# Up projection of a gated MLP: nineteen seven-product block pairs in eight column groups instead of sixteen in eleven, more split buffers, and a residual copy in eight pieces

## The chip, the cores and the metric

One core of a Trainium2 chip runs the whole kernel. The metric is device time in microseconds (us) from the start to the end of one execution. The engines named here are TensorE (PE, matrix products; PEld is its weight load), VectorE (DVE), ScalarE (ACT), GpSimd (POOL) and SyncE (SP, which here mostly issues DMA transfers). The program lists each engine's instructions in one fixed order; at an instruction whose data or buffer isn't there yet, the engine waits, and with it all that stands behind.

## The reference

One layer of a decoder trunk with 256 tokens and width 2048, in float32:

```python
h = rms_norm(x, mix_norm_g)
z = h @ w_in                                  # all heads' inputs and gates
ha = mLSTM heads(z); hb = forgetting-attention heads(z)
x = x + concat([ha, hb]) @ w_out              # out projection, 2048 x 2048
h = rms_norm(x, ffn_norm_g)
u = h @ w_up                                  # up projection, 2048 x 11264
a, g = split(u, 2)
a = causal_dwconv(a, conv_w, conv_b)          # width 3, depthwise
x = x + (gelu(a) * g) @ w_down                # down projection, 5632 x 2048
gate = sigmoid(rms_norm(x, ple_norm_g) @ w_ple_gate)
x = x + gate * (p @ w_ple_proj)
```

## The kernel before

**Products in three parts.** Every weight block arrives from HBM in float32 (`raw`). ACT rounds it to the type that the matmuls here take, fp32r (`hi`, line 1292 in the up projection, 295 elsewhere), and DVE subtracts that from the raw block (`lo`, lines 1294 and 297). The activations have been split the same way. Each product is then three matmuls (lines 362 to 364, in `three`): high by high, high by low, low by high. Such a pair of a `hi` and a `lo` is called a split here.

**The up projection in groups.** The 11264 columns are worked in 11 groups `q` = 0 to 10, each of 512 columns of the `a` half and the 512 columns of the `g` half that go with them. A group sums over 16 blocks of 128 rows of `w_up`. A *plain unit* (letter `p` in the table `ORDERS`) takes one block: one transfer of 512 KB, one split of 128x1024, 12 matmuls of 128x512. A *seven* (four units that share a letter, `a` or `b`) takes two blocks together by the seven-product scheme for 2x2 block matrices (Strassen's, in Winograd's form): 21 matmuls in place of 24. Its units have 3, 6, 6 and 6 matmuls; their splits are of 128x512, then three of 128x1024, and DVE forms four sums of raw halves (128x512 each) between them. The products that serve several result blocks gather in PSUM banks `upP`, over all the sevens of a group. At the end of a group with sevens a *combine* follows: one copy by ACT, then two additions and one subtraction on DVE (lines 1762 to 1764), and in the next group two multiply-adds (`summed`, line 1157) that join the combined halves to the plain ones. The activation side of a seven needs sums of left blocks (`S_up`, made once by `up_sums`).

`ORDERS` holds one string of letters for each group, and the units run in the order of the letters. Before, group 0 has two sevens; then groups with one and with two alternate; the last two have one each. That is 16 sevens, and all 11 groups have a combine.

**What sets the order.** `run_units` walks the units. Before the matmuls of unit `i` are listed it lists the splits of units up to `i + AHEAD_UP`, as far as split buffers are free, and the loads as far as raw buffers are free. Before there are eight split buffers (`hi0` to `hi3`, `lo0` to `lo3`) of 128x1024 each. A unit takes two, the first of a seven takes one, and both come free when its matmuls are through. Jobs of the group before (turning the result, line 200; the convolution taps and sums, lines 1176 and 1183; gelu; the product with `g`, line 1189; the split of the result, line 159; for pairs that the down projection treats as sevens their left sums, lines 467 to 471) are hung behind units of the next group, at the places in `TURN_AT` and `ACT_AT`. A scheduler that works at build time puts the instructions in their final order on each engine, by priorities and dependencies.

**The residual.** `xs` holds x after the out projection. `keep_x` copies it to HBM (`kept_x`) by two transfers of 1 MB on SP's queue (line 83): the first behind unit 8 of the second group of the out projection, the second behind unit 8 of the up projection. The out projection also loads its weights through SP (line 286), and ten moves named `mkT<-mkT` (line 206), which bring a transposed tile of the attention heads to its place, go through SP too.

Of the kernel before, what the change touches and what calls it, by code (L numbers as in the profile page):

```python
# [9 lines left out]
F32 = mybir.dt.float32  # L10
# [5 lines left out]
P = 128  # L16
# [19 lines left out]
RAW, PARTS = 3, 4  # L36
AHEAD_UP, AHEAD_LATE = 4, 6

# [19 lines left out]
@with_exitstack  # L58
def layer_kernel(
# [21 lines left out]
    def keep_x(i):  # L81
        c = slice(i * 1024, (i + 1) * 1024)
        nc.sync.dma_start(out=kept_x[:, :, c], in_=xs[:, :, c])

# [182 lines left out]
    def run_stream(blocks, pulls, more, ramp=False):  # L267
# [9 lines left out]
        def put(j):  # L277
            b = blocks[j]
            if b.load is not None:
                b.load()  # L280
            b.raws, b.tags = [], free(j)[: len(b.srcs)]
            for t, src in zip(b.tags, b.srcs):
                held.add(t)
                kb, n = src.shape[1], src.shape[2]
                raw = wp.tile([P, BLK], F32, tag=t, name=f"raw{j}", bufs=1) if t in raw_tags else more[t][2]()
                nc.sync.dma_start(out=raw[:, : kb * n].rearrange("p (k n) -> p k n", k=kb), in_=src)
                b.raws.append(raw)

# [213 lines left out]
    with mixers:  # L502
# [430 lines left out]
        def with_after(b, hook):  # L933
            fn = b.fn
            b.fn = lambda hi, lo: (fn(hi, lo), hook())
# [152 lines left out]
    with tc.tile_pool(name="ffn", bufs=1) as fp:  # L1088
# [62 lines left out]

        def up_turn():

# [7 lines left out]
            def turned(t):  # L1161
# [5 lines left out]
                return f  # L1167
            return [f(t) for t in range(NT) for f in (summed, turned)]

# [34 lines left out]
        now = [0]  # L1204
        spaces = [f"raw{i}" for i in range(RAW)] + [f"{k}{i}" for k in ("hi", "lo") for i in range(PARTS)] + ["v0", "v1", "v2", "v3", "v4"]
# [23 lines left out]
        def space(j, name, kind):  # L1229
# [7 lines left out]
            elif tag == "v4":  # L1237
                v = xs[:, 0, BLK : 2 * BLK]
            elif tag[0] == "v":
                v = spare_raws[f"u{32 + 4 * (i // 2)}"][:, i % 2]  # L1240
# [454 lines left out]
        def up_group(q):  # L1695
# [3 lines left out]

            n7 = "a" in ORDERS[q], "b" in ORDERS[q]  # L1700
            first, n7 = 2 * sum(n7), sum(n7)
            def left(k, t):
# [79 lines left out]
            us = [unit(k) for k in range(first, KD)]  # L1782
            kinds = {"p": iter(us), "a": iter(seven(0)), "b": iter(seven(1))}
            return [next(kinds[c]) for c in ORDERS[q]]

        def up_sums(r):
            f, d = (EZ[:, 0, i * 512 : (i + 1) * 512].rearrange("p (k c) -> p k c", c=256) for i in range(2))
            dve.tensor_add(f, f32(x2[:, 2 * r : 2 * r + 2, 0:256]), f32(x2[:, 2 * r : 2 * r + 2, 256:512]))
            sums_of(f, EZ[:, 1, 0:512].rearrange("p (i c) -> p i c", i=4), S_up[r])

# [28 lines left out]
        for q in range(KF // 4):  # L1819
            for job, i in zip(up_turn(), TURN_AT if q < KF // 4 - 1 else (-1, 0, -1, 1)):  # L1820
                with_after(us[START[q + 1] + i], between(job))
            for i, job in enumerate(up_act(q)):
                if q < KF // 4 - 1:
                    with_after(us[START[q + 1] + ACT_AT[i]], between(job))
                else:
                    with_after(us[first_late + 8 + 2 * i], between(job))
# [33 lines left out]
```

## Time and profile before

| What | Value |
|---|---|
| Median of 3 runs | 1232.29 us (1231.33 to 1235.31) |
| The profiled execution: own time | 1232.22 us |
| The profiled execution: span from first to last instruction | 1230.4 us |
| PE busy | 1223.2 us, 99% of the span |
| DVE busy | 1009.7 us, 82% |
| ACT busy | 757.0 us, 62% |
| Mean granted TensorE clock | 0.999 |

The profile is of one execution, and its own time stands 1.82 us above its span (what lies before the first and behind the last instruction). Busy shares are means over the whole span; a stretch of the timeline has its own.

### The profile page before, as it was taken

The page shows a single profiled execution, that of the slowest core. Times are in us where ns is not written, and L with a number is a line of the kernel's source. Part 1 is how long each engine was busy: PE and PEld are TensorE (multiplying, and loading weights), DVE is VectorE, ACT ScalarE, POOL GpSimd, SP SyncE. Part 2 cuts the span into 40 slices and gives each one's busy share as a digit, 9 for nine tenths or more (in the row PEclk, how much of TensorE's full clock was granted, in tenths as well). Part 3 has the DMA queues.
Part 4 walks back from the last instruction along what each step waited for, and adds up shares of the span by engine and source line. Part 5 has one row for each costly group of instructions (what it writes and reads, how often), then busy time and mean ns, then how long its engine had stood idle before and what let it go on. Part 6 is the DMA issues. An engine that isn't in the chain of part 4 may idle for free.

```text
span 1230.4 us, 16417 instructions
## 1 busy us (share of the span) xinstructions
PE 1223.2 (99%) x5589; PEld 1030.4 (84%) x5589; DVE 1009.7 (82%) x1262; ACT 757.0 (62%) x1109; POOL 172.9 (14%) x321
## 2 busy tenths in 40 slices
PE   9999999999999999999999999999999999999998
PEld 7999988888888788888888888888888888888887
DVE  6788857675679988788998898998788999999773
ACT  8567545565655665766676676757656656556652
POOL 2011237243301201011101100110110000050000
PEclk9999999999999999999999999999999999999999
DMA  9566587676566677767687678656797896776560
GB/s 305 182 195 196 170 235 223 186 216 188 169 229 214 197 250 244 234 217 236 208 275 241 185 250 272 224 173 221 236 304 245 302 369 207 265 252 213 194 226 35
DMA packets 127718, 276.37 MB, mean 225 GB/s; under 512 B 14682, under 2 KB 25042, under 8 KB 127634
## 3 DMA queue, kind: packets, MB, share of 16 engines
q1 hardware_dynamic: 116560, 257.73, 65.6%
q0 software_dynamic: 10688, 17.43, 5.0%
q8 instruction: 44, 0.72, 0.2%
q14 instruction: 41, 0.33, 0.1%
q10 hardware_dynamic: 385, 0.16, 0.1%
HBM read 247.99 MB, written 8.93 MB: 209 GB/s over the span
## 4 chain that ended last, share of the span: by engine, by line
PE 96%; DMA 1%; DVE 1%; issue 0%; ACT 0%; SPq 0%; ACTq 0%; DVEq 0%
PE up L364 12%; PE up L362 12%; PE up L363 11%; PE tg L351 6%; PE tg L352 6%; PE tg L353 6%; PE pg L362 4%; PE pg L363 4%; PE pg L364 4%; PE dnP L1342 1%; PE dnP L1344 1%; PE dnP L1343 1%; PE upP L363 1%; PE upP L364 1%; PE upP L362 1%; PE gt L363 1%
## 5 line engine op out<-in xcount | busy, mean ns | idle before, releaser
L363 PE MATMUL up<-part,x2T 128*128 128x512 f32 x608 | 237.0, 390 | 0.0
L364 PE MATMUL up<-part,x2T 128*128 128x512 f32 x608 | 236.6, 390 | 0.0
L1292 ACT CAST part<-raw 128x1024 fp32r<-128x1024 f32 (+1 forms) x144 | 145.9, 1022 | 109.3 <-PE up L364 34.9
L297 DVE TENSOR_TENSOR lo<-raw,hi 128x1024 fp32r<-128x1024 f32 (+3 forms) x119 | 139.2, 1172 | 78.2 <-ACT hi L295 78.0
L362 PE MATMUL up<-part,x2T 128*128 128x512 f32 x608 | 185.6, 390 | 0.0
L1294 DVE TENSOR_TENSOR part<-raw,part 128x1024 fp32r<-128x1024 f32 (+1 forms) x140 | 164.4, 1182 | 20.6 <-ACT part L1292 17.1
L295 ACT CAST hi<-raw 128x1024 fp32r<-128x1024 f32 (+3 forms) x119 | 120.0, 1010 | 99.5 <-PE tg L353 44.9
L363 PEld LDWEIGHTS up<-part,x2T 128*128 128x128 f32 x608 | 114.2, 188 | 23.6
L364 PEld LDWEIGHTS up<-part,x2T 128*128 128x128 f32 x608 | 114.2, 188 | 23.5
L362 PEld LDWEIGHTS up<-part,x2T 128*128 128x128 f32 x608 | 114.2, 188 | 23.6
L353 PE MATMUL tg<-hi,hT 128*128 128x512 f32 x288 | 113.7, 396 | 0.0
L352 PE MATMUL tg<-lo,hT 128*128 128x512 f32 x288 | 113.4, 394 | 0.0
L351 PE MATMUL tg<-hi,hT 128*128 128x512 f32 x288 | 112.5, 397 | 0.0
L206 POOL DMA_DIRECT2D EZ<-Y x66 | 35.0, 538 | 359.0 <-issue 166.6
L1292 ACT CAST part<-u36r 128x1024 fp32r<-128x1024 f32 (+1 forms) x46 | 47.8, 1042 | 35.4 <-PE up L364 17.7
L1294 DVE TENSOR_TENSOR part<-u36r,part 128x1024 fp32r<-128x1024 f32 (+1 forms) x46 | 55.6, 1209 | 10.0 <-ACT part L1292 5.8
L352 PEld LDWEIGHTS tg<-lo,hT 128*128 128x128 f32 x288 | 54.2, 188 | 10.9
L353 PEld LDWEIGHTS tg<-hi,hT 128*128 128x128 f32 x288 | 54.2, 188 | 10.9
L351 PEld LDWEIGHTS tg<-hi,hT 128*128 128x128 f32 x288 | 53.9, 188 | 10.6
L1294 DVE TENSOR_TENSOR part<-u32r,part 128x1024 fp32r<-128x1024 f32 (+1 forms) x44 | 50.4, 1148 | 12.1 <-ACT part L1292 10.5
L1292 ACT CAST part<-u32r 128x1024 fp32r<-128x1024 f32 (+1 forms) x44 | 43.4, 991 | 22.2 <-PE up L364 9.0
L363 PE MATMUL pg<-lo,hT 128*128 128x430 f32 (+1 forms) x156 | 55.8, 358 | 0.0
(936 smaller groups left out, 2765.6 us busy)
## 6 DMA issues: line engine op xcount, KB each, us to landing
raw<-in_w_up_dram SPq DMA_DIRECT2D x78, 512.0 KB, 5.1
raw<-in_w_in_dram SPq DMA_DIRECT2D x71, 512.0 KB, 4.4
u36r<-in_w_up_dram SPq DMA_DIRECT2D x43, 512.0 KB, 5.8
raw<-in_w_down_dram SPq DMA_DIRECT2D x41, 512.0 KB, 5.6
u32r<-in_w_up_dram SPq DMA_DIRECT2D x34, 512.0 KB, 4.8
xs<-in_w_up_dram SPq DMA_DIRECT2D x21, 512.0 KB, 5.1
w2b<-in_w_down_dram SPq DMA_DIRECT2D x20, 512.0 KB, 5.8
raw<-in_w_out_dram SPq DMA_DIRECT2D x17, 512.0 KB, 5.2
```

The source lines that it names most:

```text
L206: (other if other and (4 * a + b) % 3 else pool).dma_start(out=c[32 * b : 32 * b + 32, a::4], in_=y[32 * a : 32 * a + 32, :, b])
L295: act.copy(hi, raw)
L297: dve.tensor_sub(lo, raw, f32(hi))
L351: pe.matmul(o, ah, hi[:, i, :], start=first, stop=False)
L352: pe.matmul(o, ah, lo[:, i, :], start=False, stop=False)
L353: pe.matmul(o, al, hi[:, i, :], start=False, stop=last)
L362: pe.matmul(o, ah, hi, start=start, stop=False)
L363: pe.matmul(o, ah, lo, start=False, stop=False)
L364: pe.matmul(o, al, hi, start=False, stop=stop)
L1292: act.copy(r32(hi), raw)
L1294: dve.tensor_sub(r32(lo), raw, hi)
L1342: pe.matmul(o, ah, hi, start=first, stop=False)
```

## The change

1. **Where the sevens stand.** The table becomes: group 0 two sevens as before; groups 1, 3 and 5 none (16 plain units); groups 2, 4 and 6 four each (24 units: one plain, then four sevens whose units follow close on each other, one plain); then one, two, one, one. That is 19 sevens in eight groups. In groups without a seven there is neither a combine nor a `summed`.
2. **Left sums.** `S_up` for the third and fourth pair of blocks are made too, by DVE in group 1, and lie in the tile `uC`.
3. **Split buffers.** `AHEAD_UP` is 6 instead of 4, and four more split buffers `y0` to `y3` lie in the tile `uB`. They may be used for units below `START[5] + 8` = 108: in groups 1 to 4 (groups 2 and 4 are the first and the second with four sevens), not in group 6, the third with four, which has units 116 to 139.
4. **Jobs of the group before** hang at places that depend on the length of the group (`ACT_AT`).
5. **The residual copy** has eight transfers of 256 KB (rows of 1 KB instead of 4 KB): four behind units 3, 6, 9 and 12 of the second group of the out projection, four behind units 6, 8, 10 and 12 of the up projection, and each is put in order behind the load listed last.
6. The second group of the out projection has one `p` moved from behind its sevens to between their units.

```diff
-AHEAD_UP, AHEAD_LATE = 4, 6
+AHEAD_UP, AHEAD_LATE = 6, 6
...
-ORDERS = ("pppppp" "apapapap" "bpbbbp",
-          *("pppppp" "apapapap" "pppp", "ppp" "apapapap" "bpbpbpb" "pp") * 4,
-          *("pppppp" "apapapap" "pppp",) * 2)
+NONE, ONE, TWO = "p" * 16, "pppppp" "apapapap" "pppp", "ppp" "apapapap" "bpbpbpb" "pp"
+FOUR = "p" "aapaap" "bbpbb" "ccpccp" "ddpdd" "p"
+ORDERS = ("pppppp" "apapapap" "bpbbbp", NONE, FOUR, NONE, FOUR, NONE, FOUR, ONE, TWO, ONE, ONE)
...
-OUT_ORDERS = ("pppp" "apapapap" "bpbpbpb" "p", "pp" "apapapa" "bpbpbb" "ppppp")
-ACT_AT = (9, 10, 11, 12, 13, 14, 15, 16, 17, 18)
+OUT_ORDERS = ("pppp" "apapapap" "bpbpbpb" "p", "pp" "apapapap" "bpbpbb" "pppp")
+ACT_AT = {16: (6, 7, 8, 9, 10, 11, 12, 13, 14, 15), 24: (8, 9, 11, 12, 14, 15, 17, 18, 20, 21)}
+ACT_ELSE = (9, 10, 11, 12, 13, 14, 15, 16, 17, 18)
...
     def keep_x(i):
-        c = slice(i * 1024, (i + 1) * 1024)
-        nc.sync.dma_start(out=kept_x[:, :, c], in_=xs[:, :, c])
+        c = slice(i * 256, (i + 1) * 256)
+        with tc.issue_after(last["load"]):
+            nc.sync.dma_start(out=kept_x[:, :, c], in_=xs[:, :, c])
...
-                with_after(grp[8], lambda: keep_x(0))
+                for i in range(4):
+                    with_after(grp[3 + 3 * i], lambda i=i: keep_x(i))
...
+        S_up += [uC[:, 2 * i : 2 * i + 2].rearrange("p k (x c) -> p (k x) c", c=256) for i in range(2)]
...
-            return [f(t) for t in range(NT) for f in (summed, turned)]
+            return [f(t) if f is turned or with_z else (lambda: None) for t in range(NT) for f in (summed, turned)]
...
-        splits = (*spaces[RAW : RAW + 2 * PARTS], "w0", "w1", "w2", "w3")
+        splits = (*spaces[RAW : RAW + 2 * PARTS], "y0", "y1", "y2", "y3", "w0", "w1", "w2", "w3")
...
+                if t[0] == "y":
+                    return j < START[5] + 8
...
-        with_after(us[8], between(lambda: keep_x(1)))
+        for i in range(4):
+            with_after(us[6 + 2 * i], between(lambda i=i: keep_x(4 + i)))
...
-        for r, i in enumerate((2, 9)):
+        for r, i in enumerate((2, 9, START[1] + 3, START[1] + 5)):
             with_after(us[i], between(lambda r=r: up_sums(r)))
```

In the orders below a number behind a tile's name tells instances apart, `part_0_` and `part_1_` begin the names of a `hi` and a `lo`, and the `lo` bears the number of its `hi` plus one.

**DVE, end of group 6.** Before, this is a group with two sevens. 6504 is the `lo` of the last unit of the second seven, 6526 and 6537 those of the two plain units behind it, 6556 belongs to group 7.

```order
L1294 TENSOR_TENSOR part_1_6471<-raw_0_6234,part_0_6470 128x1024
L1183 TENSOR_TENSOR xs<-Y,xs 128x4x255
L1294 TENSOR_TENSOR part_1_6504<-xs,part_0_6503 128x1024
L1183 TENSOR_TENSOR xs<-Y,xs 128x4x254
L1294 TENSOR_TENSOR part_1_6526<-u32r,part_0_6525 128x1024
L1294 TENSOR_TENSOR part_1_6556<-u36r,part_0_6555 128x1024
L1762 TENSOR_TENSOR xs<-upP_6429,xs 128x512
L1294 TENSOR_TENSOR part_1_6537<-u32r,part_0_6536 128x1024
L1189 TENSOR_TENSOR xs<-xs,EZ 128x1024
L1763 TENSOR_TENSOR xs<-upP_6404,xs 128x512
```

In the changed kernel group 6 is the third with four sevens. 6463 and 6473 are the `lo`s of the third and the last unit of its fourth seven, 6487 that of its last plain unit, 6507 and 6527 those of the first two units of group 7.

```order
L1303 TENSOR_TENSOR part_1_6487<-xs,part_0_6486 128x1024
L1759 TENSOR_TENSOR u36r<-u36r,raw_0_6295 128x512
L1303 TENSOR_TENSOR part_1_6463<-raw_0_6295,part_0_6462 128x1024
L1194 TENSOR_TENSOR xs<-xs,EZ 128x1024
L1760 TENSOR_TENSOR u36r<-u36r 128x512
L1303 TENSOR_TENSOR part_1_6507<-raw_0_6368,part_0_6506 128x1024
L470 TENSOR_TENSOR Sf<-xs 128x2x128
L159 TENSOR_TENSOR uB<-xs,uB 128x4x256
L471 TENSOR_TENSOR Sf<-Sf,xs 128x128
L1303 TENSOR_TENSOR part_1_6527<-raw_0_6397,part_0_6526 128x1024
L472 TENSOR_TENSOR Sf<-xs,Sf 128x128
L1303 TENSOR_TENSOR part_1_6473<-u36r,part_0_6472 128x1024
```

Behind the last unit of the last seven there is now one plain unit instead of two, and the `lo` of that last seven's unit (6473) stands behind the `lo`s of three plain units, that of the third unit of its seven, and seven other instructions (sums of raw halves at 1759 and 1760, a product at 1194, the split of a result at 159, left sums at 470 to 472).

**PE, the same place.** Before, the last unit of the second seven (6503, 6504) and the first of the two plain units behind it alternate:

```order
L362 MATMUL upP_6429<-part_0_6503,S_up_4103 128x512
L362 MATMUL up_6261<-part_0_6503,x2T_3875 128x512
L362 MATMUL up_6260<-part_0_6525,x2T_4245 128x512
L362 MATMUL up_6262<-part_0_6525,x2T_4245 128x512
L362 MATMUL up_6263<-part_0_6525,x2T_4245 128x512
L363 MATMUL upP_6429<-part_1_6504,S_up_4103 128x512
L364 MATMUL upP_6429<-part_0_6503,S_up_4103 128x512
L363 MATMUL up_6261<-part_1_6504,x2T_3875 128x512
L364 MATMUL up_6261<-part_0_6503,x2T_3875 128x512
L362 MATMUL up_6261<-part_0_6525,x2T_4245 128x512
```

In the changed kernel, from the first matmul that reads 6463 on:

```order
L366 MATMUL upP_6272<-part_1_6463,uC 128x512
L367 MATMUL upP_6272<-part_0_6462,uC 128x512
L366 MATMUL upP_6276<-part_1_6463,uC 128x512
L367 MATMUL upP_6276<-part_0_6462,uC 128x512
L366 MATMUL up_6570<-part_1_6507,x2T_3876 128x512
L367 MATMUL up_6570<-part_0_6506,x2T_3876 128x512
L365 MATMUL up_6570<-part_0_6526,x2T_3876 128x512
L366 MATMUL up_6570<-part_1_6527,x2T_3876 128x512
L367 MATMUL up_6570<-part_0_6526,x2T_3876 128x512
L365 MATMUL upP_6284<-part_0_6472,uC 128x512
L365 MATMUL up_6196<-part_0_6472,x2T_3876 128x512
L366 MATMUL upP_6284<-part_1_6473,uC 128x512
```

The first matmuls of group 7 (bank `up_6570`) are now listed between the third and the last unit of the fourth seven. 32 matmuls stand from the one that frees the buffer of 6486 (the last to read 6434, row 3148 of PE's order; it is `up_6197<-part_0_6434,uC`) to the first that reads 6527, and 36 to the first that reads 6473.

**DVE, end of group 2**, the first with four sevens, changed kernel. 5143 is the `lo` of its last plain unit; the rows with `uB` as output at lines 1303 are `lo`s in the new split buffers.

```order
L1303 TENSOR_TENSOR part_1_5102<-xs,part_0_5101 128x1024
L1303 TENSOR_TENSOR part_1_5111<-raw_0_4978,part_0_5110 128x1024
L1760 TENSOR_TENSOR u36r<-u36r 128x512
L1303 TENSOR_TENSOR part_1_5123<-raw_0_5010,part_0_5122 128x1024
L1303 TENSOR_TENSOR part_1_5143<-u32r,part_0_5142 128x1024
L1303 TENSOR_TENSOR uB<-u36r,uB 128x1024
L1194 TENSOR_TENSOR xs<-xs,EZ 128x1024
L1303 TENSOR_TENSOR uB<-u36r,uB 128x1024
L470 TENSOR_TENSOR Sf<-xs 128x2x128
L1771 TENSOR_TENSOR xs<-upP_4929,xs 128x512
```

Here the splits stand ahead of the jobs of the group before, which begin with the product at line 1194.

**SP, end of the out projection.** Before:

```order
L83 DMA kept_x<-xs 256x1x1024
L286 DMA raw_3818<-in_w_out_dram 128x1024
L206 DMA mkT<-mkT 32x2x128 x10
L286 DMA raw_3846<-in_w_out_dram 128x1024
L286 DMA morex_3390<-in_w_out_dram 128x1024
L286 DMA morex_3393<-in_w_out_dram 128x1024
L286 DMA raw_3861<-in_w_out_dram 128x1024
L286 DMA raw_3937<-in_w_out_dram 128x1024
```

In the changed kernel:

```order
L288 DMA raw_3818<-in_w_out_dram 128x1024
L85 DMA kept_x<-xs 256x1x256
L208 DMA mkT<-mkT 32x2x128 x10
L288 DMA raw_3847<-in_w_out_dram 128x1024
L288 DMA morex_3390<-in_w_out_dram 128x1024
L288 DMA raw_3862<-in_w_out_dram 128x1024
L288 DMA morex_3393<-in_w_out_dram 128x1024
L85 DMA kept_x<-xs 256x1x256
L288 DMA raw_3923<-in_w_out_dram 128x1024
L85 DMA kept_x<-xs 256x1x256 x2
```

The first of two 1 MB copies stood ahead of the ten moves; of the four small ones that take its place one stands there, and three stand between and behind the last loads.

More of the change, by code (lines that the diff above doesn't have):

```diff
@@ L286, in put @@
                 nc.sync.dma_start(out=raw[:, : kb * n].rearrange("p (k n) -> p k n", k=kb), in_=src)
+                last["load"] = traced()
                 b.raws.append(raw)
@@ L1204, in layer_kernel @@
         now = [0]
-        spaces = [f"raw{i}" for i in range(RAW)] + [f"{k}{i}" for k in ("hi", "lo") for i in range(PARTS)] + ["v0", "v1", "v2", "v3", "v4"]
+        spaces = [f"raw{i}" for i in range(RAW)] + [f"{k}{i}" for k in ("hi", "lo") for i in range(PARTS)] + ["v0", "v1", "v2", "v3", "v4", "y0", "y1", "y2", "y3"]
         until = {"v0": 8, "v1": 8, "v2": 9, "v3": 9}
-        splits = (*spaces[RAW : RAW + 2 * PARTS], "w0", "w1", "w2", "w3")
+        splits = (*spaces[RAW : RAW + 2 * PARTS], "y0", "y1", "y2", "y3", "w0", "w1", "w2", "w3")
         held, used = set(), {}
@@ L1238, in space @@
                 v = xs[:, 0, BLK : 2 * BLK]
+            elif tag[0] == "y":
+                v = f32(uB[:, 2 * i : 2 * i + 2]).rearrange("p k c -> p (k c)")
             elif tag[0] == "v":
@@ L1698, in up_group @@
             st = {}
-            n7 = "a" in ORDERS[q], "b" in ORDERS[q]
-            first, n7 = 2 * sum(n7), sum(n7)
+            n7 = len(set(ORDERS[q]) - {"p"})
+            first = 2 * n7
             def left(k, t):
@@ L1782, in up_group @@
             us = [unit(k) for k in range(first, KD)]
-            kinds = {"p": iter(us), "a": iter(seven(0)), "b": iter(seven(1))}
+            kinds = {"p": iter(us), **{c: iter(seven(r)) for r, c in enumerate("abcd"[:n7])}}
             return [next(kinds[c]) for c in ORDERS[q]]
         def up_sums(r):
-            f, d = (EZ[:, 0, i * 512 : (i + 1) * 512].rearrange("p (k c) -> p k c", c=256) for i in range(2))
-            dve.tensor_add(f, f32(x2[:, 2 * r : 2 * r + 2, 0:256]), f32(x2[:, 2 * r : 2 * r + 2, 256:512]))
-            sums_of(f, EZ[:, 1, 0:512].rearrange("p (i c) -> p i c", i=4), S_up[r])
+            if r < 2:
+                w, f = EZ[:, 0], EZ[:, 1]
+            else:
+                v = fp.tile([P, BLK], F32, tag="pT", name="Sd_up")
+                w, f = v[:, 0:512], v[:, 512:1024]
+            d = w[:, 0:512].rearrange("p (k c) -> p k c", c=256)
+            dve.tensor_add(d, f32(x2[:, 2 * r : 2 * r + 2, 0:256]), f32(x2[:, 2 * r : 2 * r + 2, 256:512]))
+            sums_of(d, f[:, 0:512].rearrange("p (i c) -> p i c", i=4), S_up[r])
         us = []
```

7 lines of the change are left out of this document (4 added, 3 removed).

## The prediction

> **What bounds the kernel now.** I read the page's busy shares first, then its shares of the chain that ended last, then the chain itself in order of time around the groups that change.
>
> ```profile
> PE 1223.2 (99%) x5589; PEld 1030.4 (84%) x5589; DVE 1009.7 (82%) x1262; ACT 757.0 (62%) x1109; POOL 172.9 (14%) x321
> PE 96%; DMA 1%; DVE 1%; issue 0%; ACT 0%; SPq 0%; ACTq 0%; DVEq 0%
> 512.51 0.68 PE up L362 x3
> ...
> 597.51 0.68 PE up L362 x3
> ```
>
> PE is busy for 99% of the span, and 96% of the last chain runs on it: the matmuls are the bound, and whatever is taken off PE shortens the span as long as PE is fed. The two chain rows are the starts of two groups of the up projection with the same number of sevens, two groups apart. A pair with one and two sevens has 18 + 20 units and (192 - 3) + (192 - 6) = 375 matmuls; 85.00 us / 375 = 0.2267 us for a matmul. That is the price on PE. (A row's own 0.39 us, below, overlaps its neighbours.)
>
> The table by stage (columns: window, length, PE, PEld, DVE, ACT and POOL with instructions, granted clock, DMA share, GB/s) says what is near the bound beside it; its first row is the end of the out projection, the others are two such pairs of groups.
>
> ```profile
> 400.00:420.00 20.00, 19.10 (x85) 15.49 (x84) 17.73 (x21) 13.16 (x16) 6.84 (x13) 1.00 0.70 217
> 512.50:597.50 85.00, 85.00 (x377) 70.44 (x376) 75.20 (x77) 57.68 (x78) 6.91 (x13) 1.00 0.73 229
> 597.50:682.50 85.00, 85.00 (x377) 70.44 (x376) 76.31 (x81) 57.90 (x78) 7.55 (x14) 1.00 0.75 235
> ```
>
> PE has no gap in the up projection. DVE is at 88 to 90% there, ACT at 68%, the transfers at 73 to 75%. The one gap between the front and the tail lies in the first row, 0.9 us.
>
> **The sevens on PE.** Three more sevens save 3 x 3 matmuls: 9 x 0.2267 = 2.04 us less, on the path. Where the other sixteen stand is nothing to PE by itself.
>
> **DVE, the second engine.** Its rows overlap, so I take the step from one start to the next in a busy stretch:
>
> ```profile
> 643.14 0.29 DVE L468 TENSOR_TENSOR Sf<-Sf,xs 128x128 f32<-128x128 f32 x1
> 643.35 1.22 DVE L1764 TENSOR_TENSOR xs<-upP,xs 128x1024 f32<-128x1024 f32 x1
> ...
> 645.81 2.48 DVE L1157 SCALAR_TENSOR_TENSOR EZ<-xs,rstd_ffn,EZ 128x1024 f32<-128x1024 f32 x2
> 648.21 0.69 DVE L471 TENSOR_TENSOR Sp<-Sf,Sp 128x512 fp32r<-128x512 f32 x1
> 648.81 2.37 DVE L200 STREAM_TRANSPOSE Y<-EZ 128x1024 f32<-128x1024 f32 x2
> 651.10 1.19 DVE L1294 TENSOR_TENSOR part<-u32r,part 128x1024 fp32r<-128x1024 f32 x1
> ...
> 713.16 1.22 DVE L1294 TENSOR_TENSOR part<-u36r,part 128x1024 fp32r<-128x1024 f32 x1
> 714.29 0.69 DVE L1751 TENSOR_TENSOR xs<-xs 128x512 f32<-128x512 f32 x1
> 714.89 1.22 DVE L1294 TENSOR_TENSOR part<-raw,part 128x1024 fp32r<-128x1024 f32 x1
> 716.03 1.22 DVE L1183 TENSOR_TENSOR xs<-Y,xs 128x1020 f32<-128x1020 f32 x1
> 717.16 1.22 DVE L1294 TENSOR_TENSOR part<-xs,part 128x1024 fp32r<-128x1024 f32 x1
> ...
> 726.82 0.42 DVE L467 TENSOR_TENSOR Sf<-xs 128x256 f32<-128x256 f32 x1
> 727.16 1.22 DVE L1294 TENSOR_TENSOR part<-raw,part 128x1024 fp32r<-128x1024 f32 x1
> ```
>
> Steps: 1.13 us at 128x1024 (713.16 to 714.29), 0.60 at 512, 0.33 at 256, 0.21 at 128, 1.20 for a multiply-add, 1.15 for a transpose. A seven costs DVE 3 x 1.13 + 0.60 for the `lo`s and 4 x 0.60 for the half sums, 6.39, against 2 x 1.13 for two plain units: 4.13 more, 12.4 for three. A combine with its multiply-adds is 2 x 0.60 + 1.13 + 2 x 1.20 = 4.73; three groups lose theirs, 14.2 less. Two more sets of left sums are some 2 x 1.9 (0.60, 0.33, two of 0.21, 0.60). Net +2 us, off the path; what counts is each stretch:
>
> A group without sevens holds 16 x 1.13 + 4.73 (the combine of the group before) + 2 x 1.15 + 5.9 (two tap sums, product, result split at 1.13 each, left sums 1.35) = 31 us on DVE against 192 x 0.2267 = 43.5 on PE: plenty of air. A group with four holds 4 x 6.39 + 8 x 1.13 + 2 x 1.15 + 5.9 = 42.8 against 180 x 0.2267 = 40.8: DVE is 2.0 us short in each of the three, and that must come out of the lead it has on PE. By the same count a group before had 39.3 with two sevens (PE 42.2) and 35.1 with one (PE 42.8), 74.4 for the pair; the table shows 75.2 to 76.3.
>
> These rows, from DVE's timeline, also show how long the lead is for the last unit of a second seven: its `lo` (717.16, above) ends at 718.38, and PE comes to it at 721.56 (PE's timeline and ACT's):
>
> ```profile
> 721.56 0.39 PE L363 MATMUL upP<-part,S_up 128*128 128x512 f32 x1
> 712.01 1.05 ACT L1292 CAST part<-u36r 128x1024 fp32r<-128x1024 f32 x1 [0.80 <-PE up L364]
> ```
>
> 3.2 us of lead. The second row shows how the lead is made: the rounding waits for PE to free a buffer, takes 1.05, and the `lo` starts 1.15 after it (713.16).
>
> **The third group with four sevens (group 6)** has only the eight old buffers. By the orders shown, the buffer for unit 6486 is freed by PE's row 3148. From there PE has 32 matmuls to the first that needs the `lo` 6527, 7.25 us, and 36 to the one that needs 6473, 8.16 us. In that time: 0.39 for that matmul, 1.15 until the `lo` 6487 starts, and DVE's nine steps before 6527 (1.13, 0.60, 1.13, 1.13, 0.60, 1.13, 0.33, 1.13, 0.20) = 7.38, then 1.22 for 6527: 10.14 us, 2.9 late. 6473 follows 1.33 later, 11.47, 3.3 late in all. Here the split that PE wants stands behind jobs; PE stops for both, and what lies behind it (group 7's matmuls) moves by as much. I take +3.3. Bounds: 0, if PE frees that buffer earlier against its later rows than I count, and 3.3 + 2.0 = 5.3, if DVE's shortage of 2.0 stands on top.
>
> **The first two groups with four (groups 2 and 4)** have twelve buffers. The buffer comes free two units sooner, 12 matmuls or 2.7 us, and in DVE's order the `lo`s stand ahead of the product, the split and the left sums (3.0 us in the sum above). 3.3 - 2.7 - 3.0 leaves a margin of 2.4, against the shortage of 2.0. I take 0; bounds 0 and 3.3 each. The margin is thin, and it is the first rival.
>
> **Other work of the change.** ACT gets four more roundings of about a microsecond and loses three copies; at 68% in the stretch it hides them. The number of weight transfers stays.
>
> ```profile
> raw<-in_w_up_dram SPq DMA_DIRECT2D x78, 512.0 KB, 5.1
> ```
>
> They land in 5.1 us and the groups with four pull their 16 blocks in 40.8 us instead of 42 to 43: 0, bounds 0 and 1.
>
> **The residual copy and the end of the out projection.** The 0.9 us gap is this, by PE's waits (first row), PE's timeline, the chain (the late load and the rounding behind it), SP's timeline and the DMA issues of that stretch:
>
> ```profile
> PE pg L362 <- ACT hi L295: 0.9, 1, 0.9
> 414.25 0.39 PE L364 MATMUL pg<-hi,catT 128*128 128x512 f32 x1
> 415.53 0.96 PE L362 MATMUL pg<-hi,catT 128*128 128x512 f32 x3 [0.90 <-ACT hi L295]
> ...
> 404.24 9.14 DMA raw<-in_w_out_dram
> ...
> 414.44 1.05 ACT hi L295
> ...
> 392.39 0.62 SPq L83 DMA_DIRECT2D kept_x<-xs  x1
> 395.88 6.50 SPq L206 DMA_DIRECT2D mkT<-mkT  x10
> 402.47 0.53 SPq L286 DMA_DIRECT2D raw<-in_w_out_dram  x1
> ...
> kept_x<-xs SPq DMA_DIRECT2D x1, 1024.0 KB, 4.6
> ```
>
> 1.28 us between two starts instead of 0.23: 1.05 lost. The rounding had no block to work on, since the load issued at 404.24 took 9.14 us to land; SP could not issue it before its ten moves (395.88 to 402.4) were through. The page names ACT, but the late one is the transfer. In the new order five loads still stand behind the ten moves, so the gap's cause stays: 0. Bounds: -1.05, if taking 768 KB of the copy from ahead of the moves lets SP start them sooner, and 3 x 0.62 = +1.9, if the three pieces among the last loads hold SP up. The eight pieces themselves move the same 2 MB; at a DMA share of 0.70 they are hidden, and nothing waits for `kept_x` before the tail.
>
> The Trainium skill, "DMA: Bandwidth & Descriptors", section Bandwidth, part Measured, speaks against the smaller pieces: it asks to batch transfers to at least 1 MiB, and for loads issued by another engine gives 341 GB/s at 1 MB and 138 at 64 KB. By that, 2 MB would take between 6.2 and 15.2 us of transfer time (my estimate); no run so far shows a 256 KB copy, and the free share of the transfers would hide either.
>
> **The sum.** 1230.4 - 2.04 + 3.3 = 1231.7 of span; around the span the profiled execution had 1232.22 - 1230.4 = 1.82: **1233.5 us**. That execution is 0.07 below the median of the runs, so it stands for them. 0.3%, what a measurement of this kernel can tell from no change, is 3.7 us: the forecast is "the same".
>
> **Rivals.**
>
> *All three starve (slower).* The same late `lo`s cost 3.3 in groups 2 and 4 too: 1230.4 - 2.04 + 3 x 3.3 + 1.82 = 1240.1. For it: 42.8 against 40.8 on DVE, and a margin of 2.4 against 2.0. Against: twelve buffers and the order of the rows. It decides where DVE falls more than 2.4 us behind the freed buffers. Chance 0.13.
>
> *The lead holds everywhere.* No stall in group 6 either, since my chain charges DVE every row in series from one release: 1230.2. For it: the 3.2 us of lead before nearly equals the 3.3. Against: it was with two plain units behind the last seven, now there is one. With the out projection's gap gone too, 1229.1. Chance 0.17.
>
> *The pieces delay the last loads of the out projection.* Three pieces are 768 KB, 3/4 of a copy that took 4.6 us: up to 3.5 on top, 1237.0. For it: that place already ends in a late transfer. Against: a 0.70 share. Chance 0.09.
>
> *The clock falls in the stall.* A stop of 3.3 us, three times the longest seen in this stretch, lets the granted clock drop; one plain unit (12 matmuls) at half speed then costs 2.7 more: 1236.2. Against: the clock is 1.00 in the row of 400 to 420, across the 1.05 us stop. Chance 0.06. The Trainium skill, "TensorE: Matmul & The Clock Gate", Part 1, has such a rule: after an idle window of about 3.4 us the clock is halved until PE has been busy about as long. That row agrees as far as it goes; the stop forecast here is just at that rule's edge, and no run so far shows one so long.
>
> **Range and chances.** My forecast's case has 0.55 (1232 to 1235.5). The range goes down to the case with no stall and no gap, 1228.9 with a little for the spread of the runs, and up to 1238.5: stalls of part of the first rival's size, or the third or fourth rival's. Left out is the first rival at its full price, most of its 0.13. Slower than 1236.0: the first rival, half of the third, over half of the fourth, 0.21. Faster than 1228.6: only the best end of the second, 0.04. The rest is 0.75.
>
> **What would show it.** In the profile after: nine matmuls fewer; PE without gaps in groups 2 and 4; PE stopped twice at the end of group 6, some 3 us together, released by DVE's `lo` line, with the stopped matmuls those of the first units of group 7 and the last unit of the fourth seven; the out projection's gap near 1 us, behind a late load; clock 1.00 throughout. I am wrong if PE stops in groups 2 or 4, if DVE is idle while PE is stopped in group 6, or if the loads land much later.

## The result, and the profile after

The changed kernel takes 1240.36 us in the median of 6 runs (1238.57 to 1241.19), the kernel before 1231.94 in 6 runs beside them: a ratio of 1.0061 (95% interval 1.0047 to 1.0075), slower by about 7.5 us by the ratio (8.4 by the medians). The prediction was 1233.5, "the same", with a range up to 1238.5: the median lies above it. The profiled execution is the fastest of the six: 1238.57 us, span 1236.8, clock 0.999.

The page of the changed kernel, busy times and shares of the last chain:

```profile
PE 1224.2 (99%) x5580; PEld 1027.3 (83%) x5580; DVE 1011.4 (82%) x1275; ACT 761.2 (62%) x1114; POOL 175.7 (14%) x321
PE 94%; DMA 2%; DVE 2%; ACT 1%; issue 1%; SPq 0%; DVEq 0%; ACTq 0%
```

PE has nine instructions fewer (5589 to 5580), as worked out, and the busy shares hardly move. The chain tells more: two points that were PE's now belong, as rounded, to transfers, DVE, ACT and the engines' own issuing. Which waits they are, PE's waits from 395 us to 1000 us say (waited for, us in total, times, longest):

```profile
PE up L366 <- DVE part L1303: 2.3, 3, 0.9
PE up L365 <- ACT part L1301: 1.5, 2, 0.8
PE up L366 <- DVE uB L1303: 1.5, 1, 1.5
PE up L365 <- ACT uB L1301: 0.9, 1, 0.9
PE pg L365 <- ACT hi L298: 0.9, 1, 0.9
PE upP L366 <- DVE part L1303: 0.3, 1, 0.3
```

Before, the fifth of these was the only one. The others lie at three places. Below, the loss at a place is the step between two starts less the usual 0.23.

**The start of the up projection**, 3.4 us (1.07, 1.62 and 0.73), in the table by stage (the columns are those of the prediction's table), then on PE's timeline:

```profile
427.00:433.00 6.00, 3.64 (x15) 2.40 (x14) 5.66 (x7) 5.62 (x11) 0.00 (x0) 1.00 0.88 292
...
428.93 1.20 PE L365 MATMUL up<-uB,x2T 128*128 128x512 f32 x4 [0.91 <-ACT uB L1301]
431.58 0.50 PE L366 MATMUL up<-uB,x2T 128*128 128x512 f32 x1 [1.45 <-DVE uB L1303]
...
441.53 0.50 PE L366 MATMUL up<-part,x2T 128*128 128x512 f32 x1 [0.56 <-DVE part L1303]
```

**The end of group 6**, 3.5 us (1.07, 0.94, 1.08, 0.43), where it was forecast. PE's timeline, then DVE's:

```profile
728.32 0.50 PE L366 MATMUL up<-part,x2T 128*128 128x512 f32 x1 [0.91 <-DVE part L1303]
729.82 0.49 PE L365 MATMUL up<-part,x2T 128*128 128x512 f32 x1 [0.77 <-ACT part L1301]
731.13 0.50 PE L366 MATMUL up<-part,x2T 128*128 128x512 f32 x1 [0.82 <-DVE part L1303]
732.60 0.51 PE L366 MATMUL upP<-part,uC 128*128 128x512 f32 x1 [0.26 <-DVE part L1303]
...
727.05 1.22 DVE L1303 TENSOR_TENSOR part<-raw,part 128x1024 fp32r<-128x1024 f32 x1
728.18 0.42 DVE L470 TENSOR_TENSOR Sf<-xs 128x256 f32<-128x256 f32 x1
728.52 1.22 DVE L159 TENSOR_TENSOR uB<-xs,uB 128x1024 fp32r<-128x1024 f32 x1
729.65 0.28 DVE L471 TENSOR_TENSOR Sf<-Sf,xs 128x128 f32<-128x128 f32 x1
729.86 1.22 DVE L1303 TENSOR_TENSOR part<-raw,part 128x1024 fp32r<-128x1024 f32 x1
```

DVE works without a break there: PE waits for the low part that begins at 727.05, then for the one at 729.86, with the job at 728.52 (the split of group 5's result) between the two. By PE's order these are, in turn, the `lo` 6507, the rounding 6526, the `lo` 6527 and the `lo` 6473.

**Group 10**, 0.87 us and some small change:

```profile
893.71 0.50 PE L365 MATMUL up<-part,x2T 128*128 128x512 f32 x1 [0.71 <-ACT part L1301]
888.13 1.05 ACT L1301 CAST part<-xs 128x1024 fp32r<-128x1024 f32 x1 [2.27 <-DMA xs<-in_w_up_dram]
```

Here ACT waited for a load, and seven instructions further, with no break between, the rounding that PE needs (892.62) came late. 3.4 + 3.5 + 0.9 = 7.8. The profiled span shows 8.4: it is 6.4 longer with 2.04 of matmuls gone. The other 0.6 is what two small effects leave: the step behind a stop is 0.34 instead of 0.23, at most of them, and this execution was 0.4 ahead of the kernel before when it came to the gap in the out projection (415.15 against 415.53).

**The clock.** The other five executions are 1.1 to 2.6 us longer, at a mean clock of 0.997 or 0.998. Two more profiles of the changed kernel (a1 and a2 below) show where such time goes. Of a1, by stage:

```profile
428.19:431.60 3.41, 1.59 (x6) 0.67 (x4) 3.41 (x5) 3.35 (x7) 0.00 (x0) 1.00 1.00 321
431.60:435.01 3.41, 2.96 (x7) 2.38 (x8) 1.53 (x2) 1.23 (x4) 0.00 (x0) 0.50 0.95 323
435.01:438.40 3.39, 3.39 (x17) 2.78 (x17) 0.15 (x1) 2.10 (x2) 0.00 (x0) 1.00 1.04 397
728.56:731.97 3.41, 1.23 (x3) 0.48 (x3) 3.41 (x5) 3.41 (x6) 0.00 (x0) 1.00 0.71 241
731.97:735.38 3.41, 3.25 (x8) 2.56 (x9) 2.42 (x5) 0.93 (x2) 0.55 (x1) 0.50 0.65 210
735.38:738.80 3.42, 3.42 (x17) 2.81 (x16) 3.35 (x4) 2.57 (x3) 0.00 (x0) 1.00 0.87 246
```

The column behind POOL is the granted clock: 1.00, then 0.50 for 3.41 us behind each of the two places, with 7 and 8 matmuls in a time that has 17 just behind, and 1.00 again. In the profiled execution above, the same stops left it at 1.00.

Matmul by matmul (all three profiles have the same 5580 in the same order), a1 and a2 fall behind that execution by 0.5 and 0.6 us across the start of the up projection, where the third stop (0.73) is gone with PE at half speed, and by 0.9 each across the end of group 6. Another 0.5 and 0.3 had come in the first 30 us, far ahead of the up projection.

### The profile page after: what moved, and what is told of

The parts are those of the page before. It is cut to its first block, busy times and chain, and to the rows that moved or that the text cites. A ratio compares the mean times of both kernels' runs of the same rounds, so it can differ in the third digit from the quotient of the medians.

```text
span 1236.8 us, 16407 instructions
## 1 busy us (share of the span) xinstructions
PE 1224.2 (99%) x5580; PEld 1027.3 (83%) x5580; DVE 1011.4 (82%) x1275; ACT 761.2 (62%) x1114; POOL 175.7 (14%) x321
## 4 chain that ended last, share of the span: by engine, by line
PE 94%; DMA 2%; DVE 2%; ACT 1%; issue 1%; SPq 0%; DVEq 0%; ACTq 0%
PE up L366 10%; PE up L367 10%; PE up L365 10%; PE tg L354 6%; PE tg L355 6%; PE tg L356 6%; PE pg L365 5%; PE pg L366 4%; PE pg L367 4%; PE upP L366 1%; PE upP L367 1%; PE upP L365 1%; PE dnP L1353 1%; PE dnP L1351 1%; PE dnP L1352 1%; DVE part L1303 1%
## 5 line engine op out<-in xcount | busy, mean ns | idle before, releaser
L366 PE MATMUL up<-part,x2T 128*128 128x512 f32 x491 | 191.6, 390 | 2.3 <-DVE part L1303 2.3
L1301 ACT CAST part<-raw 128x1024 fp32r<-128x1024 f32 x131 | 131.8, 1015 | 95.0 <-PE up L367 19.1
L367 PE MATMUL up<-part,x2T 128*128 128x512 f32 x487 | 189.5, 389 | 0.0
L1303 DVE TENSOR_TENSOR part<-raw,part 128x1024 fp32r<-128x1024 f32 (+1 forms) x125 | 145.8, 1172 | 36.6 <-ACT part L1301 32.5
L365 PE MATMUL up<-part,x2T 128*128 128x512 f32 x487 | 159.8, 390 | 1.5 <-ACT part L1301 1.5
L366 PEld LDWEIGHTS up<-part,x2T 128*128 128x128 f32 x491 | 92.2, 188 | 22.9 <-DVE part L1303 3.9
L365 PEld LDWEIGHTS up<-part,x2T 128*128 128x128 f32 x487 | 91.3, 188 | 21.1 <-ACT part L1301 2.3
L367 PEld LDWEIGHTS up<-part,x2T 128*128 128x128 f32 x487 | 91.4, 188 | 18.9
L367 PE MATMUL pg<-hi,hT 128*128 128x430 f32 (+1 forms) x156 | 55.6, 356 | 0.0
L1301 ACT CAST part<-u36r 128x1024 fp32r<-128x1024 f32 (+1 forms) x40 | 40.1, 1006 | 24.1 <-PE up L367 14.2
L1303 DVE TENSOR_TENSOR part<-u36r,part 128x1024 fp32r<-128x1024 f32 (+1 forms) x40 | 46.6, 1164 | 9.2 <-ACT part L1301 7.9
L1301 ACT CAST part<-u32r 128x1024 fp32r<-128x1024 f32 (+1 forms) x37 | 37.4, 1015 | 26.4 <-PE up L367 9.5
```

Source lines behind the costliest of these rows:

```text
L365: pe.matmul(o, ah, hi, start=start, stop=False)
L366: pe.matmul(o, ah, lo, start=False, stop=False)
L367: pe.matmul(o, al, hi, start=False, stop=stop)
L1301: act.copy(r32(hi), raw)
L1303: dve.tensor_sub(r32(lo), raw, hi)
```

## The experiments

All are changes to the changed kernel unless said otherwise; "start" and "group 6" are the places above. Each but a1 and a2 was timed in five rounds beside the kernel before, whose medians were 1231.6 to 1231.9.

**e1: new buffers from unit 8 on.**

```diff
-                    return j < START[5] + 8
+                    return 8 <= j < START[5] + 8
```

> The changed kernel, but the four new split buffers may be used from unit 8 on, so that units 0 to 7 split into the eight old ones. Theory A (the new buffers lie in a tile whose memory the out projection's last combine still uses as scratch, and being unused so far they are picked first for units 0 and 1): the three PE gaps at the start of the up projection (1.07, 1.62 and 0.73 us lost) go, the time falls by 3 to 4 us plus what the clock lost there. Rival B (the copy in eight pieces and the other order of the out projection bring the first loads late): the gaps stay, time as the changed kernel within 1 us. The end of group 6 (3.5 to 4 us lost) stays with both.

1241.44 us, ratio 1.0075 (1.0062 to 1.0088). The three stops at the start are gone, and a new one stands 20 us later, PE's longest:

```profile
PE upP L365 <- DVE x2T L162: 2.8, 1, 2.8
```

The first units are cured, so the buffers had to do with it, and not the late loads by themselves: the third unit's load is as late as in the changed kernel (4.8 us ahead of the last matmul of the out projection, at 428.33; 4.9 there), and PE doesn't stop for it. It is the first of these two:

```profile
423.50 3.86 SPq L1278 DMA_DIRECT2D raw<-in_w_up_dram  x2
```

But the build-time order that comes of it put a piece of the activations' transposing (`x2T`) late on DVE, and that took the gain back. Group 6 lost as before, with the half clock behind it.

**e2, e5 and e6: the residual copy and the out projection's second order, both or one undone.**

```diff
 # e2: both;  e5: only the copy;  e6: only the order
-            for i in range(4): with_after(grp[3 + 3 * i], lambda i=i: keep_x(i))    # 256 KB each
+            with_after(grp[8], lambda: keep_x(0))                                   # 1 MB, and so for the second
-OUT_ORDERS = (..., "pp" "apapapap" "bpbpbb" "pppp")
+OUT_ORDERS = (..., "pp" "apapapa" "bpbpbb" "ppppp")
```

> The changed kernel with the residual copy in two pieces of 1 MB and the out projection's second order as before. Theory A: the start gaps of the up projection stay (over 3 us), time as the changed kernel within 1 us. Rival B: they go, 3 to 4 us faster.

> The changed kernel with the residual copy in two pieces of 1 MB; the out projection's second order stays new. e2 undid both and the start of the up projection lost 0.9 us on PE instead of 3.4. Theory C (the eight pieces hold up the last loads): as e2, start loses about 1 us, 1237 us. Theory D (the moved plain unit changes which block takes which raw buffer, and so when the first loads of the up projection may start): start loses 3 us or more, 1239 to 1241 us.

> The changed kernel with the out projection's second order as before; the copy stays in eight pieces. Theory C: start loses 3 us or more, 1239 to 1241 us. Theory D: start loses about 1 us, 1237 us.

e2: 1237.2 us, 1.0040 (1.0027 to 1.0054). e5: 1242.47, 1.0081 (1.0066 to 1.0096). e6: 1239.19, 1.0058 (1.0044 to 1.0072). PE's waits for the new buffers at the start, e2, e5 and e6 in this order:

```profile
PE up L365 <- DVE uB L1301: 0.7, 1, 0.7
...
PE up L365 <- DVE uB L1301: 2.0, 1, 2.0
PE up L364 <- ACT uB L1299: 0.9, 1, 0.9
...
PE up L366 <- DVE uB L1303: 2.1, 1, 2.1
PE up L365 <- ACT uB L1301: 0.4, 1, 0.4
```

Undoing both saves 2.6 us by the ratios. Undoing either leaves the start as it was: its first two stops lose 3.2 us in e5 and 2.8 in e6, 2.7 in the changed kernel. Neither of the two theories in the expectations holds: each edit alone is enough. What they share is when the third unit's load is issued, 6.5 us ahead of the last matmul of the out projection in the kernel before and in e2, 5.5 in e5, 5.2 in e6, 4.9 in the changed kernel (422.77 against 427.64). In each of them it is issued 0.03 us after DVE is through with the last raw block of the out projection (its last `lo` ends at 421.38 in the kernel before and at 422.74 in the changed one), so it waits for that, and that block now comes later. Why the build places it so with either edit was not traced.

**e4: the kernel before with only the four new buffers and splits six units ahead.**

> The kernel before with only the four new split buffers (for units below 98) and splits six units ahead. Theory A: PE loses 3 to 4 us at the start of the up projection, 1235 to 1237 us, the rest as before. Rival B: as before within 1 us, or faster.

1232.41 us, 1.0002 (0.9994 to 1.0010). The time is as rival B has it, the mechanism as theory A: a stop comes, but of 0.8 us, not 3 to 4, and 0.8 is less than these runs can tell from none.

```profile
PE pg L362 <- ACT hi L295: 0.7, 1, 0.7
PE up L363 <- DVE uB L1298: 0.7, 1, 0.7
...
425.07 1.05 ACT L1296 CAST part<-raw 128x1024 fp32r<-128x1024 f32 x1 [4.13 <-DMA raw<-in_w_up_dram]
426.02 2.00 ACT L1296 CAST uB<-raw 128x1024 fp32r<-128x1024 f32 x2
```

ACT's rows show how: `part<-raw` is the rounding of the third unit, and the two into `uB` behind it are those of the first and the second. ACT waits 4.13 us for the third unit's load, while the two units that PE needs first stand behind it. In the changed kernel the same load is later still, and so is everything behind it:

```profile
422.77 0.54 SPq L1278 DMA_DIRECT2D raw<-in_w_up_dram  x1
426.88 1.05 ACT L1301 CAST part<-raw 128x1024 fp32r<-128x1024 f32 x1 [4.32 <-DMA raw<-in_w_up_dram]
427.84 1.98 ACT L1301 CAST uB<-raw 128x1024 fp32r<-128x1024 f32 x2
```

In the kernel before, the first unit's rounding began at 420.19.

**e9 and e10: the new buffers from unit 2 on**, so that the first two units split into old ones; e10 changes nothing else, e9 is e7 (below) with it.

```diff
-                    return j < START[5] + 8
+                    return 2 <= j < START[5] + 8
```

> The changed kernel with the new split buffers from unit 2 on, nothing else. Theory E: the stops at the first two units (1.07 and 1.62 us) go; a stop of under 1 us at unit 2 may stay. The end of group 6 keeps its 3.5 to 4 us. 1237 to 1238.5 us. Rival: the late raw buffers of the out projection hold the start up in any case, and the stops come back at the next units as in e1: 1240 us or more.

> e7 (18 sevens, old copy, old out projection) with the new split buffers from unit 2 on. Theory E: at the start of the up projection PE waits because the rounding of unit 2 stands ahead of those of units 0 and 1 on ACT (they go to the new buffers, which come free late), and unit 2's load is the last to arrive. Units 0 and 1 in old buffers: the 0.9 us lost at the start go, 1230.4 to 1230.8 us. If the late load itself is what PE waits for, the stop moves to unit 2 and the time stays 1231.3.

e10: 1238.86 us, 1.0057 (1.0045 to 1.0070). The start is clean (the table by stage, at the place that showed 3.64), and ACT's rows give the reason that the new buffers are late:

```profile
427.00:433.00 6.00, 6.00 (x28) 4.99 (x27) 6.00 (x10) 2.75 (x4) 0.00 (x0) 1.00 0.67 207
...
425.99 2.00 ACT L1301 CAST part<-raw 128x1024 fp32r<-128x1024 f32 x2 [0.90 <-DMA raw<-in_w_up_dram]
429.99 1.05 ACT L1301 CAST uB<-raw 128x1024 fp32r<-128x1024 f32 x1 [1.99 <-DVE xs L1064]
```

The first rounding into `uB` waits for DVE at line 1064. That line is the last to read `mqT`, a tile that the out projection's last combine uses as scratch, and `uB` is placed over its memory. So the new buffers can't be had before the out projection's last combine, about when the up projection begins, and an allocator that prefers what was used longest ago gives these, never used, to the first two units. (In the changed kernel line 1064 is through at 426.13, and what ends last is the third unit's load, for the rounding at 426.88.) That is the start, shown. The time says less: it fell by only 0.5 us by the ratios (1.5 by the medians), to just above what was expected. In the profile, matmul by matmul, the start gives 3.8 us against the changed kernel's; 1.1 comes back as stops of 0.55 us at the ends of groups 2 and 4 and 1.1 as half clock behind group 6. And the first 12 us had cost 2.5 more, with the clock at 0.50 from 8.0 to 11.4 us, where this edit changes nothing. (The profiles of e6, e11 and e13 have such a stretch too, from 7.4 to 8.3 us on.)

e9: 1232.5 us, 1.0011 (1.0002 to 1.0020), and not the 1230.4 to 1230.8 that were expected: the 0.9 at the start went, 1.8 came elsewhere (0.55 at groups 2 and 4, 0.7 in group 10).

**e3: no third group of four. e7: the same with both edits of e2.**

```diff
-ORDERS = (..., NONE, FOUR, NONE, FOUR, NONE, FOUR, ONE, TWO, ONE, ONE)
+ORDERS = (..., NONE, FOUR, NONE, FOUR, ONE, TWO, ONE, TWO, ONE, ONE)
```

> The changed kernel with groups 5 and 6 as one and two sevens instead of none and four: 18 sevens. If the third group of four starves for want of the four new buffers and of DVE time (3.5 to 4 us lost at its end), that stop goes for 3 more matmuls (0.68): 2.8 to 3.3 us faster than the changed kernel. If the stop comes from elsewhere (late loads, PSUM banks), a stop of over 2 us stays at the end of group 6, and the time is the same or 0.7 longer. The start gaps stay.

> e2 (old copy, old out projection) with groups 5 and 6 as one and two sevens (18 sevens, two groups of four). If start, end of group 6 and the clock are separate losses that add: before 1231.9, less 6 matmuls (1.36), plus the 0.9 at the start: 1231.4, within 1 us of before. If a stop that the other edits hid comes up, over 1233.

e3: 1234.6 us, 1.0019 (1.0010 to 1.0028), 5.2 us less than the changed kernel by the ratios. No stop is left from group 1 on, neither in group 6 nor in group 10; the gain is larger than expected, by as much as the half clock behind group 6 and the stop in group 10 can explain, which no run separates. e7: 1231.31 us, 0.9998 (0.9989 to 1.0007), within what was expected; PE's only waits are

```profile
PE pg L364 <- ACT hi L297: 1.0, 1, 1.0
PE up L365 <- DVE uB L1301: 0.8, 1, 0.8
```

Two groups of four, with twelve buffers each, run without a stop; the six matmuls that they save (1.36 us) are mostly paid back at the start.

**e8: e2 with the new buffers only up to unit 67**, so that group 4 has the eight old ones, as group 6 has.

```diff
-                    return j < START[5] + 8
+                    return j < START[3] + 8
```

> e2 with the four new split buffers only for units below START[3] + 8 = 68, so that group 4 (the second with four sevens) has the eight old ones, as group 6 has. If the missing buffers make the stop at the end of group 6: group 4 loses 3 to 4 us at its end too, 1240 to 1241.5 us. If it is something of group 6 alone (the group of one seven behind it, left sums): group 4 stays without a stop, time as e2 (1237.2) within 1 us.

1243.57 us, 1.0095 (1.0081 to 1.0110). PE's waits and two windows at the end of group 4, then e2 in the first of them:

```profile
PE up L365 <- DVE part L1301: 3.4, 4, 0.9
PE up L364 <- ACT part L1299: 1.5, 2, 0.8
...
638.00:644.00 6.00, 3.69 (x14) 2.17 (x12) 6.00 (x8) 4.36 (x6) 0.00 (x0) 1.00 0.73 236
644.60:647.40 2.80, 2.80 (x8) 2.09 (x8) 1.87 (x3) 0.35 (x1) 0.55 (x1) 0.50 0.59 184
...
638.00:644.00 6.00, 6.00 (x28) 4.99 (x27) 5.55 (x7) 3.57 (x5) 0.00 (x0) 1.00 0.85 286
```

Group 4 now stops as group 6 does, DVE busy throughout, the half clock behind it, though its own work is what it was in e2. Here the number of split buffers decides, not DVE's time in the group and not what stands behind group 6.

**e13: e2 with one plain unit of group 6 moved to its end.**

```diff
-NONE, FOUR, ONE, TWO, ONE, ONE
+NONE, "p" "aapaa" "bbpbb" "ccpccp" "ddpdd" "pp", ONE, TWO, ONE, ONE
```

> e2 with one plain unit of the third group of four moved from between its first seven's units to the end, so that two stand behind the last seven. If the row order there makes the stop (the last seven's low part behind jobs and other units' low parts), it falls from 3.5 us to under 1 and no half clock follows: about 1233. If eight buffers are too few for four sevens at any order, stops of 2 us or more stay in group 6: 1235.5 to 1237.5.

1237.22 us, 1.0044 (1.0031 to 1.0056), as e2. The stop at the end of the group fell to 0.3 us, and two others stand between its sevens, without a half clock behind them:

```profile
705.49 0.73 PE L364 MATMUL upP<-part,S_up 128*128 128x512 f32 x2 [1.57 <-ACT part L1299]
712.34 0.50 PE L364 MATMUL upP<-part,uC 128*128 128x512 f32 x1 [1.51 <-ACT part L1299]
```

The row order says where PE stops, the eight buffers that it stops: 3.7 us in all here, some 3.5 in e2. The time is e2's although the half clock behind group 6 is gone. This profile has one at 8.3 us in its place, far ahead of the edit; what the other executions had is not known.

**e11 and e12: 20 sevens, never more than two in a group from group 5 on (e11) or from group 1 on (e12)**, both otherwise as e9.

```diff
 # e11
+ORDERS = (..., NONE, FOUR, NONE, FOUR, TWO, TWO, TWO, TWO, ONE, ONE)
 # e12
+ORDERS = (..., TWO, TWO, TWO, TWO, TWO, TWO, TWO, TWO, ONE, ONE)
```

> e9 with two sevens in each of groups 5 to 8: 20 sevens, 12 matmuls fewer than before (2.72 us). By the count of DVE's work a group with two sevens behind one with two needs 39.3 us on DVE against 42.2 on PE, so it is fed: 1229 to 1229.8 us. If eight split buffers or the raw buffers don't carry two such groups in a row, stops at their ends of 1 us or more each, 1232 or more.

> e9 with two sevens in each of groups 1 to 8, no group with none or four: 20 sevens as e11, but with all combines. If DVE's time in a group is what counts (39.3 against 42.2), as e11: 1229 to 1229.8 us. If the lead is used up over eight such groups, stops in groups 5 to 8, 1232 or more.

e11: 1233.61 us, 1.0017 (1.0009 to 1.0026). e12: 1238.68 us, 1.0060 (1.0046 to 1.0073). PE's waits for low parts, of e11 and of e12:

```profile
PE up L365 <- DVE part L1301: 2.1, 3, 0.8
...
PE up L365 <- DVE part L1301: 5.6, 5, 1.8
```

By the count that the prediction used, these groups need 39.3 us of DVE against 42.2 of PE, and yet PE stops in all three of them in e11 that follow another (0.8 to 0.9 us each), and six times in e12 (0.8 to 2.0 us, the first at 571.76). A sum over a group doesn't tell whether PE is fed. Nor does the number of buffers alone: units below 108 have twelve of them, and the first two stops of e12 (571.76 and 616.15) lie there. Why these groups stop was not traced.

**e15: e7 with the new buffers from unit 4 on.**

> e7 with the new split buffers from unit 4 on (e9 had them from unit 2 on, and got stops of 0.55 us at the ends of groups 2 and 4 and 0.7 in group 10). The 0.9 us at the start are gone as in e9. If the stops at the ends of groups 2 and 4 hang on which buffers rotate to which units, they may be absent: 1230.3. If barring the first units brings them in any case: 1232 to 1232.5 as e9.

1231.33 us, 0.9998 (0.9989 to 1.0007). The 0.9 at the start went, and 0.55 came back at the ends of groups 2 and 4 each, without the stop in group 10 of e9. No version here is measurably faster than the kernel before.

**a1 and a2: the changed kernel again, one profile each.**

> The changed kernel once more, for its profile. If the granted clock falls behind its stops in most executions, rows with a clock near 0.5 for about 3 us stand behind the stop at 430 or that at 728, and the span is 1 to 3 us over 1236.8. If the profile shows 1.00 throughout behind the stops, the spread has another cause.

> As the run before it: the changed kernel once more, for its profile.

1240.24 us (span 1238.5) and 1239.67 us (span 1238.0). Both show the half clock behind both stops, for 3.4 us each; a1's rows stand above. The rival, a spread from another cause, has a part: the 0.5 and 0.3 us of the first 30 us.

## Why the prediction was wrong

Of the 6.9 us between the forecast and the median, 3.4 lie at the start of the up projection, 0.9 in group 10, 0.2 in group 6, 0.6 in small delays, and 1.8 between the profiled execution and the median.

**The sevens on PE: right.** Nine matmuls fewer; in e7, with six fewer and little else changed, the sum in matmuls, the start and the time agree within the interval.

**Group 6: right in place and cause, nearly in size.** 3.3 us forecast, 3.5 measured. The two stops that were forecast (2.9 for the `lo` 6527, 0.4 more for 6473) came as four: 1.07, 0.94 and 1.08 us, at the `lo` 6507, a rounding and 6527, make 3.1, and 6473 adds 0.43. DVE worked throughout. With what e8 and e13 add, it is the eight buffers. The clause on DVE's shortage of 2.0 us was not needed for it, and e11 and e12 show that such a sum over a group is a poor guide.

**Groups 2 and 4: right.** Taken as 0; no PE wait in either. The margin was thin, as the prediction said: with the first units barred from the new buffers (e1, e9, e10, e15), a stop of 0.55 us stands at the end of each.

**The new split buffers: the step that failed.** The prediction counted them as twelve buffers for groups 2 and 4 and priced their use ahead of that nowhere. The list of changes has them in groups 1 to 4, but the program gives them to every unit below 108, so to the units of group 0 from the first on. The prediction did not ask what their memory held when the first unit wants it. They come free only behind the out projection's last combine, and the units that get them are the first two, with the third's rounding ahead of theirs on ACT. This is a stop of 0.8 us by itself (e4) and 3.4 with the late load; without it there is none, late load or not (e10).

**The residual copy and the out projection's order: mis-sized.** They were taken as 0, because the gap in the out projection stays: it did, 1.02 us. Beside the new buffers they are worth 2.6 us (3.4 at the start against 0.8 in e2). But the rows of SP's order were read only up to the out projection's own loads. What they delay stands right behind, the first loads of the up projection: the third is issued 4.9 us ahead of the out projection's last matmul instead of 6.5. The bound of +1.9 was too low for it, and the third rival (up to 3.5) had the right end with the loads of the wrong stage. With the first two units in old buffers the same late load costs nothing (e1, e10), so this term hangs on the one above. And the pieces are only one of two ways to it: e5, with the two large copies, starts as late, and so does e6, with the pieces alone.

**Other loads: 0 was wrong by 0.9 us**, in group 10. The stop there came and went with edits elsewhere (absent in e3, e7 and e15, present in e9); what sets it was not found.

**The clock: the fourth rival, held unlikely at 0.06, takes part in the median.** The median lies 1.8 us above the profiled execution. Both extra profiles have the half clock twice; it makes them 1.4 to 1.5 us longer in all (0.5 and 0.6 at the start, 0.9 each in group 6). They lie 1.7 and 1.2 us of span above the profile without it, with 0.5 and 0.3 from the first 30 us, and with a smaller stop in group 10 (0.40 and 0.17 in place of 0.87). The Trainium skill, "TensorE: Matmul & The Clock Gate", Part 1: The HAM clock gate, says that the clock is halved after an idle window of about 3.4 us, until PE has been busy for about as long. The runs agree with the length (0.50 for 3.41 us), and with its remark that the window runs free, since the same stops halved the clock in two profiles and not in the third. They don't need an unbroken idle stretch: in group 6 the longest wait is 0.9 us, and in a1 PE was busy for 1.23 of the 3.41 us ahead.

**The first rival's number was right for the wrong reason.** 1240.1 was the price of three starving groups of four. One starved; the start of the stage, a load and the clock made up the rest. That it lies 0.3 from the median is luck.

## What to carry over

A new buffer is priced by when its memory comes free, not by how many there are: look up what lay there, who reads that last, and which units an allocator will give it to first. On an engine that works in order, one late load ahead of two early ones delays all three (ACT in e4 and in the changed kernel), so read the order at the seam between two stages to the end of the next stage's first loads. A sum of an engine's work over a group is no proof that the engine downstream is fed (e11, e12); a count in order from the release of a buffer to the need, as the prediction made it for group 6, came within 0.2 us.

## What was not expected of the hardware

Several short stops of 0.8 to 1.1 us each, within 4 us, were enough to halve the TensorE clock (0.50 granted for 3.41 us), in two of three profiles of the same program. In e13, two stops of 1.7 us each, 7 us apart, did not, and in e1 a single wait of 2.8 us did not. All such stretches inside the up projection, in all profiles, last 3.4 us, and one in e8 twice that (732.94 to 739.77). So what these stops cost at the end of group 6 was 3.5 us in one execution and 0.9 more in two others.
